# Value projection of all heads ahead of the attention, as seven half-size products; the r projection gated afterwards

## The chip, the cores and the metric

The kernel runs on one core of one Trainium2 chip. The metric is the device time of one launch in microseconds (us). The core has TensorE (PE in the profile; its weight loads are PEld), VectorE (DVE), ScalarE (ACT), GpSimd (POOL) and SyncE (SP), which in this kernel issues the transfers. Each engine executes its instructions in the order in which the program lists them; waits between engines go by semaphores.

## The reference, cut to what matters

One encoder block over 1024 tokens with 1024 features, all in float32:

```python
h = rmsnorm(x, norm_mix)
q, k, v, r, lr_f, lr_b, u, g_a, g_b = split(h @ w_in)     # q, k: 512 wide; v, r: 1024 wide
log_a = log_sigmoid(lr @ w_decay_up + b_decay) / 16       # one set forward, one backward
o = gla(q, k, v, log_a_f) + flip(gla(flip(q, k, v, log_a_b)))   # 4 heads, q/k 128 and v 256 wide per head
o = o * rsqrt(mean(o * o) + eps) * gla_norm * silu(r)
y_a = o @ w_branch_gla
y_b = (multiscale_pool(u) @ w_pool_group) * pool_scale
x = x + (sigmoid(g_a) * y_a + sigmoid(g_b) * y_b) @ w_out
h2 = rmsnorm(x, norm_ffn)
x = x + (silu(h2 @ w_gate) * (h2 @ w_up)) @ w_ffn_out
out = rmsnorm(x, norm_final)
```

Products are taken to float32 accuracy: each operand is split into a high part (a cast to float32r) and a low part (the difference), and three matmuls add high x high, high x low and low x high.

## The kernel before

Tokens are in tiles of 128. `mm3` issues the three matmuls of one 128-deep step and then calls `pump`, which takes the clock for all work that runs beside the products: with every step it lowers the counters of waiting pieces by the width of the step over 512 columns (below: a unit). Three lists are served: `side` (generators such as `attention`, one after the other, each `yield` naming the units until its next piece), `aside` (preparations, one job per so many units) and `put_off` (`soon`: one piece after so many units). So the order of instructions on every engine is fixed when the program is written.

The stages, in order:

1. Start. Token tiles are normalized, transposed on PE and split into `hT` (feature-major, high and low). Meanwhile the value product of head 0 runs token tile by token tile: `values` takes 8 steps of 256 columns for a tile (head 0 has 256 value columns), each step three matmuls, and `split_to` casts the sum on ACT and subtracts on DVE. `low_rank_weights` prepares the decay weights behind tile 5; tiles 6 and 7 and then the low-rank product (L449) follow.
2. Heads. For each head `project_qk` makes q and k (4 groups of 8 steps of 512 columns), then `attention(h)` begins as a side generator. It runs beside the next head's q, k and values, and for the last head beside r. Its chain: four products `z`, then on DVE a minimum (L644), on ACT Abs, Exp, Ln with an activation table load (L645, L650, L656), then per half and direction a DVE subtraction (L663), a scan (L670, L675), and the ends of it (L681); ACT Exp twice (L688, L689), DVE and POOL multiplications (L696, L697); PE transposes of keys (L714), a split of them (`kt`, L198), the state recurrence over 8 tiles (`advance`: three matmuls `kv`, L728, L733), scores, outputs `op`.
3. r. For each of 8 column tiles `feature_major` multiplies; `gated` applies Silu on ACT to the sum, transposes the attention's output on PE and multiplies on DVE (L979); results go to HBM (`ob_out`). Beside it `feature_jobs` restores `hT` (high + low) and forms the sums and differences of its quadrants that the following stages need (DVE, L600), casts (L594) and subtracts (L585); they stay in SBUF (`right`).
4. Gates (10 units of 256 columns), branch product, output product, FFN in, FFN out. All of these already use Winograd's form of Strassen's algorithm: seven products of half size in place of eight, with operand sums formed beside and result sums kept in PSUM or added on DVE. Product numbers 1 to 7 in the code are those seven; 1, 6, 7 and 4 share one PSUM sum (`UP`).

Weights come by SP from HBM (`raw`), are cast on ACT (L197, `wh`) and their low part is subtracted on POOL (L198, `wl`). PSUM has 8 banks: 3 in the pool `ps_mm`, 5 in `ps_g`. SBUF work tiles come from a pool of 39 slots of 4 KB per partition. SP's transfers go round eight semaphores: a transfer waits until the eighth before it has landed.

Of the kernel before, what the change touches and what calls it, by code (L numbers as in the profile page):

```python
# [17 lines left out]
P = 128  # L18
# [33 lines left out]
def kernel(  # L52
# [182 lines left out]
    order = []  # L235
    for h in range(HEADS):
        cols_of = [(Q0 + h * DK, DK), (K0 + h * DK, DK), (V0 + h * DV, DV)]
        order += [(w_in, KT, *c) for c in (cols_of if h else cols_of[2:] + cols_of[:2])]
    order += [(w_in, KT, R0 + j * P, P) for j in range(KT)]
    order = iter(order)  # L240
# [25 lines left out]
    mm_banks = cycle([ps_mm])  # L266
# [92 lines left out]

    load_x(0)  # L360
# [4 lines left out]
    fetch()  # L365
# [38 lines left out]
    def value_slots():  # L404
        return [(slot(F32R, (4, DV), "vh"), slot(F32R, (4, DV), "vl")) for _ in range(2)]

    v = value_slots()
# [13 lines left out]
    prepare()  # L421
    for kp, ps in enumerate(trs):
        pending.pop(0)()
        gain_and_split(ps, kp, 0, hT, g_mix)
    w = take(ahead=False)
    norm_x(2)
    norm_x(3)
    for t in range(0, NT, 2):
        if t + 4 < NT:
            begin(norms(t + 4), 1)  # L430
# [6 lines left out]
        if t + 2 < NT:  # L437
            begin(to_features(xn[(t + 2) % 4 :], t + 2, hT, g_mix), 0.5)
        values(w, v, t + 1)
        finish_side()  # L440
        if t == 4:
            low_rank_weights()
    prepare()
    lrT = slot(F32R, (2, HALF), "lrT")
    for half in range(2):
        ps = bank(ps_mm)
# [43 lines left out]

    def chunk(w, k_half, c_half, c):
        k0 = (4 * k_half + 2 * c) * P
        return w[k0 : k0 + 2 * P, c_half * HALF : (c_half + 1) * HALF].rearrange("(k p) c -> p k c", p=P)

# [48 lines left out]
    def feature_jobs(c):  # L543
        def restored(i, j):
# [7 lines left out]
        b12, job = restored(0, 1)  # L552
        yield job
        b11, job = restored(0, 0)
        yield job
        yield diff(b11, b12, b11)
        b22, job = restored(1, 1)
        yield job
        yield diff(b12, b22, b12)
        yield diff(b22, b22, b11, 6)  # L560
        yield None, b12, 7
        yield None, b11, 5
        b21, job = restored(1, 0)
        yield job
        yield diff(b21, b21, b22, 4)
# [6 lines left out]
    def beside(jobs, every, put, lag):  # L572
# [3 lines left out]
        while True:  # L576
            job = next(jobs, None)
            if not any((job, *casts, differ, *puts)):
                return
            for pair in puts.pop(0):  # L580
                nc.sync.dma_start(*pair)
            puts.append([])
            if differ:
                src, (hi, lo), dst = differ
                nc.vector.tensor_tensor(lo, src, as_f32(hi), op=ALU.subtract)  # L585
                if len(src.shape) == 2:
                    puts[-1] += [(dst[:, i, :], as_f32(t)) for i, t in enumerate((hi, lo))]
                else:
                    right.setdefault(dst, []).append((hi, lo))
            differ, cast = None, casts.pop(0)  # L590
            if cast:
                src, dst = cast
                parts = parts_for(src)
                nc.scalar.copy(parts[0], src)  # L594
                differ = src, parts, dst
            casts.append(None)
            if job:
                op, src, dst = job
                if op:
                    op()  # L600
# [17 lines left out]
    v_heads, o_heads, unscaled = {}, {}, []  # L618
    HOLD, SCORES = 4.4, 6

    def project_qk():
        q = slot(s="q")
        k = slot(s="k")
        for dst, scale in ((q, DK**-0.5), (k, 1.0)):
            w = take()
            for half in range(2):
                ps = feature_major(w, hT, half)
                nc.scalar.activation(dst[:, half, :], ps[:, :], AF.Copy, scale=scale)
        return q, k

    def attention(h, q, k):


        qe = [slot(s="qe") for _ in range(2)]
        ke = [slot(s="ke") for _ in range(2)]
        fac = {}
# [47 lines left out]
        def exponentials(half, d):  # L684
            cs, tot, e_q = zs[half, d], totals[half, d], qe[half]
# [7 lines left out]
        def apply_decay(half, d):  # L693
            f, e_q, e_k = fac[half, d], qe[half], ke[half]
# [61 lines left out]
        yield HOLD - 2  # L756
        exponentials(0, 1)
# [10 lines left out]
        while h not in v_heads:  # L768
            yield 0.5
# [80 lines left out]
    for h in range(HEADS):  # L850
        qk = project_qk()
        begin(attention(h, *qk))
        if h == 0:
            prepare_beside(map(branch_jobs, range(4)), 6)
        if h > 0:
            v = value_slots()
            w = take()
            for t in range(NT):
                values(w, v, t)
        v_heads[h] = v  # L860
# [103 lines left out]
    raw_r, oT = [], {}  # L964

    def gated(j, half, src):

        sr = t2(s="sr")
        nc.scalar.activation(sr[:, :], src, AF.Silu)
# [6 lines left out]
        if j // 2 not in oT:  # L976
            oT[j // 2] = [slot(s="o") for _ in range(2)], []
        tiles, there = oT[j // 2]
        nc.vector.scalar_tensor_tensor(  # L979
            tiles[half][:, j % 2, :], tp[:, :], g_gla[:, j : j + 1], sr[:, :], op0=ALU.mult, op1=ALU.mult  # L980
        )
        there.append((j, half))
        if len(there) == 4:
            c = j // 2 % 2
            for half, t in enumerate(tiles):
                later(ob_out[j // 4, half][:, 2 * c : 2 * c + 2, :], t[:, :, :])

    def put_by():

        if raw_r:  # L990
            gated(*raw_r.pop(0))

    BY = 3
    sums_begun = False
    for j in range(KT):
        if 2 <= j <= 4:
            load_o(j - 2)
        w = take()
# [3 lines left out]
        if j == 7:  # L1002
            gates_ahead.step()
        if j < BY:
            whole_r = slot(s="r")
        for half in range(2):
            if j >= BY and not sums_begun and (j > BY or not side):
                finish_side()
                finish_beside()
                prepare_beside([feature_jobs(0), feature_jobs(1)], 2.3)  # L1010
                sums_begun = True
            ps = feature_major(w, hT, half)
            if half == 0:
                flush()
            if j < BY:
                nc.scalar.copy(whole_r[:, half, :], ps[:, :])
                raw_r.append((j, half, whole_r[:, half, :]))
            else:
                put_by()
                gated(j, half, ps[:, :])  # L1020
            if j == KT - 1 and half == 0:
                gates_ahead.step()
    finish_beside()
# [58 lines left out]

    def weight_split(raw):
        parts = []
        for k in range(2):
            hi = wts.tile([P, HALF], F32R, tag="wh", name=name("wh"))
            lo = wts.tile([P, HALF], F32R, tag="wl", name=name("wl"))
            split_to(hi[:, :], lo[:, :], raw[:, k, :], nc.gpsimd)
            parts.append((hi[:, :], lo[:, :]))
        return parts  # L1090
# [242 lines left out]

    U_BANKS = [ps_mm] * 3 + [ps_g]
    X_BANKS = [ps_g] * 4
# [534 lines left out]
```

## Time and profile before

| | |
|---|---|
| runs | 1396.67, 1399.2, 1400.53 us, median 1399.2 |
| profiled execution | span from first to last instruction 1400.4 us, which the page gives as its time |
| PE busy | 1371.4 us (98%) |
| DVE, ACT, POOL busy | 854.4, 624.6, 750.4 us (61%, 45%, 54%) |
| transfers | 243.62 MB, mean 174 GB/s |

The page gives busy time per engine over the span, the chain of work that ended last, and groups of equal instructions by line and tile name with count, busy time, mean duration of one, and the idle time before them. Matmuls overlap in the records: the step from one start to the next, which the merged rows of the chain give (time over count), is what one costs in a stream.

### The profile page before, as it was taken

How to read it: one execution, taken by the hardware profiler on the slowest of the kernel's cores; microseconds unless marked ns; L12 is line 12 of the kernel's file. 1: busy time of each engine (PE TensorE's matmuls, PEld its weight loads, DVE VectorE, ACT ScalarE, POOL GpSimd, SP SyncE). 2: the span in 40 equal slices, each digit the busy share in tenths (PEclk: the TensorE clock that was granted, in tenths of full speed). 3: DMA queues.
4: the chain of work that ended last, by engine and by line, in shares of the span. 5: the costliest groups of instructions: out<-in, count | busy, mean ns of one | idle time of the engine just before them, and what ended most of it. 6: DMA issues, size and time to landing. Idle time of an engine off the chain costs nothing.

```text
span 1400.4 us, 18571 instructions
## 1 busy us (share of the span) xinstructions
PE 1371.4 (98%) x6677; PEld 1157.4 (83%) x6677; DVE 854.4 (61%) x1073; ACT 624.6 (45%) x1119; POOL 750.4 (54%) x558
## 2 busy tenths in 40 slices
PE   7999999999999999999999999999999999999997
PEld 6889898988888878788887888888888888888876
DVE  6256857677745975587874865556565556343363
ACT  6364655554334444455346633333333334453253
POOL 3251616132288456468665176666666667454354
PEclk9999999999999999999999999999999999999999
DMA  6212413222368667996524455554444447975461
GB/s 193 76 45 61 136 59 107 89 79 71 125 207 286 199 220 235 346 407 233 194 76 173 173 180 174 173 173 156 145 142 148 140 153 255 388 255 218 165 234 67
DMA packets 167612, 243.62 MB, mean 174 GB/s; under 512 B 10936, under 2 KB 98016, under 8 KB 167520
## 3 DMA queue, kind: packets, MB, share of 16 engines
q1 hardware_dynamic: 167520, 242.45, 51.2%
q8 instruction: 52, 0.85, 0.2%
q14 instruction: 40, 0.33, 0.1%
HBM read 164.55 MB, written 77.86 MB: 173 GB/s over the span
## 4 chain that ended last, share of the span: by engine, by line
PE 81%; DVE 7%; ACT 4%; issue 3%; POOL 2%; DMA 2%; SPq 0%; POOLq 0%; DVEq 0%; ACTq 0%
PE ps L271 73%; PE op L813 2%; POOL wl L198 1%; PE kv L271 1%; PE sc L741 1%; PE op L271 1%; DVE z L670 1%; PE yb L271 1%; PE tr L318 1%; PE ps L449 1%; PE tp L972 1%; DMA gor<-g_out 0%; DMA wor<-t_out 0%; DVE z L675 0%; DMA u_out<-uph 0%
## 5 line engine op out<-in xcount | busy, mean ns | idle before, releaser
L198 POOL TENSOR_TENSOR wl<-fs,wh 128x512 fp32r<-128x512 f32 x120 | 165.9, 1386 | 163.4 <-ACT wh L197 138.1
L271 PE MATMUL ps<-gl,wh 128*128 128x512 f32 x616 | 239.8, 389 | 0.9 <-DVE gl L1462 0.9
L271 PE MATMUL ps<-gh,wh 128*128 128x512 f32 x616 | 240.4, 390 | 0.0
L271 PE MATMUL ps<-gh,wl 128*128 128x512 f32 x616 | 239.7, 389 | 0.0
L198 POOL TENSOR_TENSOR wl<-fraw,wh 128x512 fp32r<-128x512 f32 x90 | 129.1, 1435 | 63.9 <-ACT wh L197 63.9
L271 PE MATMUL ps<-hh,wh 128*128 128x512 f32 x376 | 150.4, 400 | 0.0
L198 POOL TENSOR_TENSOR ol<-gor,oh 128x1024 fp32r<-128x1024 f32 (+1 forms) x42 | 100.3, 2394 | 93.1 <-ACT oh L197 86.0
L271 PE MATMUL ps<-hh,wl 128*128 128x512 f32 x376 | 146.9, 391 | 0.0
L271 PE MATMUL ps<-hl,wh 128*128 128x512 f32 x376 | 146.8, 390 | 0.0
L198 POOL TENSOR_TENSOR wl<-raw,wh 128x512 fp32r<-128x512 f32 x47 | 64.4, 1382 | 152.8 <-ACT wh L197 141.4
L271 PEld LDWEIGHTS ps<-gl,wh 128*128 128x128 f32 x616 | 115.7, 188 | 25.0 <-DVE gl L1462 1.3
L271 PEld LDWEIGHTS ps<-gh,wl 128*128 128x128 f32 x616 | 115.7, 188 | 24.2
L271 PEld LDWEIGHTS ps<-gh,wh 128*128 128x128 f32 x616 | 115.7, 188 | 23.6
L271 PE MATMUL ps<-oh,oh 128*128 128x512 f32 x308 | 119.9, 389 | 1.3 <-DVE x L1792 1.3
L271 PE MATMUL ps<-ol,oh 128*128 128x512 f32 x308 | 119.9, 389 | 0.2 <-DVE ol L198 0.2
L271 PE MATMUL ps<-oh,ol 128*128 128x512 f32 x308 | 119.8, 389 | 0.0
L198 POOL TENSOR_TENSOR wl<-wraw,wh 128x512 fp32r<-128x512 f32 x56 | 90.9, 1653 | 45.4 <-ACT wh L197 36.1
L198 DVE TENSOR_TENSOR ol<-wor,oh 128x1024 fp32r<-128x1024 f32 (+1 forms) x42 | 62.0, 1496 | 53.9 <-ACT oh L197 46.6
L197 ACT CAST wh<-fs 128x512 fp32r<-128x512 f32 x120 | 73.8, 615 | 28.4 <-DVE fs L882 28.3
L271 PEld LDWEIGHTS ps<-hh,wl 128*128 128x128 f32 x376 | 70.8, 188 | 15.3
L271 PEld LDWEIGHTS ps<-hl,wh 128*128 128x128 f32 x376 | 71.1, 189 | 13.5
L271 PEld LDWEIGHTS ps<-hh,wh 128*128 128x128 f32 x376 | 71.1, 189 | 13.2
(251 smaller groups left out, 3197.4 us busy)
## 6 DMA issues: line engine op xcount, KB each, us to landing
fraw<-in_w_ffn_in_dram SPq DMA_DIRECT2D x44, 512.0 KB, 6.1
gor<-g_out SPq DMA_DIRECT2D x35, 512.0 KB, 6.3
raw<-in_w_in_dram SPq DMA_DIRECT2D x48, 256.0 KB, 3.1
g_out<-s SPq DMA_DIRECT2D x44, 256.0 KB, 2.3
fraw<-in_w_in_dram SPq DMA_DIRECT2D x20, 512.0 KB, 6.5
wor<-t_out SPq DMA_DIRECT2D x20, 512.0 KB
g_out<-g SPq DMA_DIRECT2D x33, 256.0 KB, 2.6
x<-in_x_dram SPq DMA_DIRECT2D x16, 512.0 KB, 4.9
```

The source lines that it names most:

```text
L197: nc.scalar.copy(hi, src)
L198: eng.tensor_tensor(lo, src, as_f32(hi), op=ALU.subtract)
L271: nc.tensor.matmul(ps, a[i], b[j], start=first and n == 0, stop=last and n == 2, skip_group_check=onto)
L318: nc.tensor.transpose(ps[:, c], xt[:, k * P : (k + 1) * P], ident[:, :])
L449: nc.tensor.matmul(ps[:, :], lw[k // 4][:, k % 4, :, :].rearrange("p a r -> p (a r)"), hT(k, half)[i], start=k == 0 and i == 0, stop=k == ...
L670: nc.vector.tensor_tensor_scan(cs[:, :], cy, la[:, :], 0.0, op0=ALU.mult, op1=ALU.add)
L741: nc.tensor.matmul(sc[d][:, i * CH : (i + 1) * CH], chunk_of(ke, n, d), chunk_of(qe, n, d), start=True, stop=True,)
L813: nc.tensor.matmul(op[:, :DV], a, b, start=False, stop=j == len(terms) - 1)
L972: nc.tensor.transpose(tp[:, i * P : (i + 1) * P], o_heads[j // 2][half][:, i, (j % 2) * P : (j % 2 + 1) * P], ident[:, :],)
```

## The change

The value product moves ahead of the attention for all four heads together, as one 1024 x 1024 x 1024 product in seven products of half size.

- Products 1 and 2 use weights as they are in memory and the first half of the tokens. They take the place of `values` in the start (`early`, 4 token tiles, each 4 steps of 512 columns per product). Product 1's sums stay in PSUM (three banks of `ps_mm`, one of `ps_g`) and are copied; `first_block` adds product 2 to the copy, which finishes one quadrant of the values.
- Then the low-rank product and q, k of head 0, half by half. `low_rank_weights` now stands behind the last `first_block`. Beside the second half `feature_jobs` starts (DVE): the sums of weight blocks in place, and the sums of `hT`.
- Then products 5, 3, 6, 7, 4 in that order (`VALUES`), each 2 parts of 4 token tiles and 2 steps. 6, 7 and 4 add on top of product 1's sums, so each must wait until `out_values` has read the sum before (DVE add), has cast it (ACT) and made its low part (DVE). `attention` of head 0 begins with product 6.
- The finished values go to HBM as high and low parts (`v_out`), and each head loads its own (`load_values`, 4 transfers) in the middle of its attention.
- The split feature sums that were made for products 5, 6, 7, 4 also go to HBM (`t_out_h`) and are loaded again just before the gates (`load_right`, 16 transfers of 512 KB).
- r is projected without its gate: r 0 to 2 behind q, k of head 2, r 3 to 7 behind head 3. r 0 to 5 go to HBM. A side generator `gating` begun after r 6 loads r and the attention outputs, applies Silu to a whole r tile and does what `gated` did.

The diff, cut to its core:

```diff
-    def values(w, v, t):
-        ps = bank(ps_mm)
-        for kt in range(KT):
-            mm3(ps[:, :DV], tokens(hT(kt, t // 4), t), w(kt), kt == 0, kt == KT - 1)
-        split_to(*(part[:, t % 4, :] for part in v[t // 4]), ps[:, :DV])
+    def early(p, t, w):
+        ps = U.setdefault(t, bank(U_BANKS[t])) if p == 1 else bank(ps_g)
+        for k in range(4):
+            mm3(ps[:, :], tokens(hT(k + 4 * (p == 2), 0), t), w[k], k == 0, k == 3)
+        return ps
...
+    def first_block(t, p1, hi, lo):
+        ps = early(2, t, w2)[:, :]
+        m = t % 2
+        nc.vector.tensor_tensor(ps, ps, p1[:, m, :], op=ALU.add)
+        nc.scalar.copy(hi[:, m, :], ps)
+        nc.vector.tensor_tensor(lo[:, m, :], ps, as_f32(hi[:, m, :]), op=ALU.subtract)
...
-        values(w, v, t + 1)
+        hi, lo = slot(F32R, s="vh"), slot(F32R, s="vl")
+        for m in range(2):
+            first_block(t + m, p1, hi, lo)
         finish_side()
-        if t == 4:
-            low_rank_weights()
+        soon(2, partial(store_values, 0, t, hi, lo))
+    low_rank_weights()
...
+    def first_qk(half):
+        if half == 0:
+            begin(to_features(xn[2:], 6, hT, g_mix), 2)
+        else:
+            finish_side()
+            prepare_beside([feature_jobs()], 1.5, 6)
+        low_rank(half)
+
+    qk = [project_qk(first_qk)]
+    VALUES = (5, 3, 6, 7, 4)
...
+    def out_values(i, half, m, ps, s=None):
+        hi, lo = v_parts[i, half][m // 2]
+        m2 = m % 2
+        if s is not None:
+            add(lo[:, m2, :], ps, s[:, m2, :])
+            ps = lo[:, m2, :]
+        nc.scalar.copy(hi[:, m2, :], ps)
+        def low():
+            nc.vector.tensor_tensor(..., ps, as_f32(hi[:, m2, :]), op=ALU.subtract)
+        soon(1.5, low)
+        if m2:
+            soon(5, partial(store_values, i, 4 * half + m - 1, hi, lo))
...
+    for at, p in enumerate(VALUES):
+        if p == 5:
+            x_banks = [bank(pool) for pool in X_BANKS]
+        elif p == 6:
+            begin(attention(0, *qk[0]))
+        sums = x_banks if p in (5, 3) else [U[m] for m in range(4)]
+        for c in range(2):
+            n = 2 * at + c
+            while len(split_v) <= n:
+                next_values()
+            next_values()
+            for m in range(4):
+                for k in range(2):
+                    mm3(sums[m][:, :], tuple(t[:, k, m * P : (m + 1) * P] for t in data), split_v[n][k], ...)
...
-    for h in range(HEADS):
-        qk = project_qk()
-        begin(attention(h, *qk))
-        if h > 0:
-            v = value_slots()
-            w = take()
-            for t in range(NT):
-                values(w, v, t)
-        v_heads[h] = v
+    for h in range(1, HEADS):
+        q, k = project_qk()
+        begin(attention(h, q, k))
+        if h == 2:
+            for j in range(3):
+                project_r(j)
...
+    def load_right(p):
+        right[p] = []
+        for c in range(2):
+            parts = [slot(F32R, s=s)[:, :, :] for s in ("trh", "trl")]
+            for i, t in enumerate(parts):
+                nc.sync.dma_start(as_f32(t), t_out_h[p][:, c, i])
+            right[p].append(parts)
+
+    for j in range(3, KT):
+        project_r(j)
         if j == 6:
             for _ in range(2):
                 gunits[0].load()
+            finish_beside()
+            begin(gating())
...
+    for p in (5, 6, 7, 4):
+        load_right(p)
```

More of the change, by code (lines that the diff above doesn't have):

```diff
@@ L693, in apply_decay @@
         def apply_decay(half, d):
+            if half not in ke:
+                ke[half] = slot(s="ke")
             f, e_q, e_k = fac[half, d], qe[half], ke[half]
@@ L756, in attention @@
         yield HOLD - 2
+        while h // 2 not in values_out:
+            yield 0.5
+        load_values(h)
         exponentials(0, 1)
@@ new lines, with project_r @@
+    settle()
+    finish_beside()
+    right.clear()
+    mm_banks = cycle([ps_mm])
+    prepare_beside(map(branch_jobs, range(4)), 6)
+    KEPT, kept = 6, {}
+    r_out = [dram.tile([P, 2, HALF], F32, name=f"r_out{j}") for j in range(KT)]
+    def project_r(j):
+        w = take()
+        r = slot(s="r")
+        for half in range(2):
+            ps = feature_major(w, hT, half)
+            if half == 0:
+                flush()
+            nc.scalar.copy(r[:, half, :], ps[:, :])
+        if j < KEPT:
+            later(r_out[j], r[:, :, :])
+        else:
+            kept[j] = r
@@ L1001 @@
                 gunits[0].load()
-        if j == 7:
+            finish_beside()
+            begin(gating())
+        elif j == 7:
             gates_ahead.step()
[L1004 to L1023, printed above, removed]
+            gates_ahead.step()
+    while len(side) > 1:
+        next(side[0][0], None) is None and side.pop(0)
+    for p in (5, 6, 7, 4):
+        load_right(p)
     for p, i, half in ((1, 0, 0), (2, 1, 0), (3, 1, 1)):
@@ L1081, in weight_load @@
         return raw
[L1083 to L1090, printed above, removed]
     def data_split(src):
```

271 lines of the change are left out of this document (188 added, 83 removed).

## The prediction

> **What bounds the kernel now.** I read the page's first part, the chain that ended last, the chain in order of time, and then the stretches in which the change works.
>
> ```profile
> span 1400.4 us, 18571 instructions
> PE 1371.4 (98%) x6677; PEld 1157.4 (83%) x6677; DVE 854.4 (61%) x1073; ACT 624.6 (45%) x1119; POOL 750.4 (54%) x558
> PE 81%; DVE 7%; ACT 4%; issue 3%; POOL 2%; DMA 2%; SPq 0%; POOLq 0%; DVEq 0%; ACTq 0%
> ```
>
> PE is the bound, and 81% of the chain is matmuls. Busy PE is not PE at its peak, so I take the step between starts from streams without a gap (start, time, instruction, count):
>
> ```profile
> 38.98 6.11 PE ps L271 x51
> 334.23 0.88 PE tp L972 x8
> 390.44 78.92 PE ps L271 x348
> ```
>
> A matmul with 256 columns costs 6.11/51 = 119.8 ns, one with 512 columns 78.92/348 = 226.8 ns, a transpose 0.88/8 = 0.11 us. The last stream runs 79 us without a break, so what is taken off PE comes off the time, unless a wait takes its place. Around the change PE hardly waits, but DVE is nearly full in the middle of an attention (columns: stretch, its length, PE, PEld, DVE, ACT, POOL busy, clock, DMA share, GB/s):
>
> ```profile
> 52.00:74.00 22.00, 22.00 (x99) 18.22 (x98) 0.69 (x1) 4.45 (x8) 5.08 (x4) 1.00 0.37 108
> 84.00:102.00 18.00, 18.00 (x103) 15.72 (x102) 15.01 (x24) 11.81 (x25) 13.13 (x11) 1.00 0.15 45
> PE kv L271 <- DVE kt L198: 3.4, 3, 2.1
> ```
>
> The first row is q and k of head 0 alone, the second attention 0, DVE busy 15.0 of 18 us. The third, from the waits of PE between 74 and 325 us, is its largest there: 3.4 us in three waits for DVE.
>
> **The change, part by part.**
>
> *Less PE work.* The values were 8 tiles x 4 heads x 8 steps x 3 = 768 matmuls of 256 columns; their rows:
>
> ```profile
> L271 PE MATMUL ps<-wh,hh 128*128 128x256 f32 x256 | 79.9, 312 | 0.0
> L271 PE MATMUL ps<-wl,hh 128*128 128x256 f32 x256 | 73.3, 286 | 0.5 <-POOL wl L198 0.5
> L271 PE MATMUL ps<-wh,hl 128*128 128x256 f32 x256 | 73.0, 285 | 0.0
> ```
>
> Now 7 products x 4 tiles x 4 steps x 3 = 336 matmuls of 512 columns. 768 x 0.1198 = 92.0, 336 x 0.2268 = 76.2: **-15.8 us**. Everything else on PE stays in number.
>
> *New preparations.* The rows that price them (busy, mean ns; then idle before):
>
> ```profile
> L600 DVE TENSOR_TENSOR hs<-hs,hs 128x1024 f32<-128x1024 f32 x8 | 11.8, 1481 | 0.2
> L600 DVE TENSOR_TENSOR hs<-hh,hl 128x1024 f32<-128x1024 f32 x8 | 10.7, 1351 | 0.0
> L585 DVE TENSOR_TENSOR trl<-hs,trh 128x1024 fp32r<-128x1024 f32 x8 | 10.6, 1342 | 8.6 <-DMA ob_out<-o 5.6 <-ACT trh L594 3.1
> L644 DVE TENSOR_SCALAR la<-z,cols 128x512 f32<-128x512 f32 x16 | 11.7, 746 | 22.4 <-PE z L641 22.4
> L663 DVE TENSOR_TENSOR la<-la,z 128x512 f32<-128x512 f32 x16 | 10.8, 678 | 7.7 <-ACT z L656 7.7
> L670 DVE TENSOR_TENSOR_SCAN z<-carry,la 128x512 f32<-128x512 bf16 x8 | 14.4, 1802 | 0.3
> L675 DVE TENSOR_TENSOR_SCAN z<-la,carry 128x511 f32<-128x511 f32 x8 | 13.8, 1731 | 0.3
> L681 DVE TENSOR_TENSOR z<-z,tot 128x256 f32<-128x256 f32 x16 | 6.9, 432 | 0.5
> L696 DVE TENSOR_TENSOR ke<-z,k 128x512 f32<-128x512 f32 x16 | 10.9, 680 | 0.0
> L198 DVE TENSOR_TENSOR kt<-kp,kt 128x512 fp32r<-128x512 f32 x16 | 11.0, 691 | 16.3 <-ACT kt L197 16.3
> 402.34 0.68 DVE L1256 TENSOR_TENSOR ga<-ps,ga 128x512 f32<-128x512 f32 x1
> L197 ACT CAST wh<-raw 128x512 fp32r<-128x512 f32 x48 | 28.8, 620 | 1.2 <-DMA raw<-in_w_in_dram 1.2
> L645 ACT ACTIVATE z<-z,cols 128x512 f32<-128x512 f32 x16 | 10.5, 662 | 9.1 <-DVE la L644 8.9
> L650 ACT ACTIVATE z<-z 128x512 f32<-128x512 f32 x16 | 8.2, 582 | 0.0
> L594 ACT CAST trh<-hs 128x1024 fp32r<-128x1024 f32 x8 | 8.1, 1048 | 18.9 <-DMA ob_out<-o 8.3 <-PE tp L972 6.5 <-DVE hs L600 4.2
> L656 ACT ACT_TABLE_LOAD x4 | 5.1, 1283 | 0.1
> L628 ACT ACTIVATE k<-ps 128x512 f32<-128x512 f32 x8 | 4.8, 595 | 10.9 <-PE ps L271 10.9
> L399 ACT CAST lw<-lraw 128x384 fp32r<-128x384 f32 x2 | 0.9, 530 | 0.0
> L198 POOL TENSOR_TENSOR wl<-raw,wh 128x512 fp32r<-128x512 f32 x47 | 64.4, 1382 | 152.8 <-ACT wh L197 141.4 <-issue 8.4 <-PE kv L271 3.0
> ```
>
> *Start.* PE begins behind the same chain of POOL subtractions. It now has 24 matmuls of 512 columns before it wants token tile 2, not of 256, but that tile's transfer stands behind twice the weights: -2 to +3, I take **-1**.
>
> *Low-rank weights, now behind the last value sum.* The low-rank product waits for a DVE addition (0.68), the cast (0.6, as L628), the low part (0.69, while ACT casts `lw`, 0.53) and the low part of `lw` (0.28, an estimate from L681's size): 2.25, with four handovers **+2.5** (1.5 to 3). Before, tiles 6 and 7 covered it.
>
> *First weights of product 5.* Their casts stand on ACT behind the last k sum, and nothing is split ahead: k 0.6, cast 0.62, two POOL subtractions 2 x 1.38 = 3.98, then two more matmuls, 4.4 with handovers, where four token tiles could have had 1.36 for the first: **+3.1** (2 to 3.5). Later weights are one part (5.4 us) ahead and POOL needs 2.8, so they cost nothing.
>
> *Products 6, 7 and 4 beside attention 0.* Here I expect the loss. Product 7 may not add to a PSUM sum before DVE has read product 6's, and product 4 likewise; those additions stand on DVE between the attention's instructions. From the first `la` to the last addition that product 4 waits for, DVE has 4 la (3.0), 4 subtractions (2.7), 4 scans (7.1) with ends (1.7 + 0.7), 3 ke (2.0), 1 kt (0.7), and newly 4 low parts of feature sums (5.4), 8 additions (5.4) and 6 low parts of values (4.1): 32.9 us. PE without waits reaches that point 10.9 (product 6) + 10.9 (7) + 4.1 (three tiles of 4) + 4 z (0.9), 8 transposes (0.9) and 3 kv (0.4) = 28.1 us after product 6 began. DVE also comes late by some 2.5 us: the feature and weight sums (24 pieces of 1.35 to 1.48, 8 low parts of 1.34 in all) occupy it from the low-rank product on. So 2.5 + 32.9 - 28.1 = 7.3 us if DVE never waited. It does wait: its low parts need casts that stand on ACT behind 4 Abs (2.6), 4 Exp (2.3), 4 Ln (2.3, as L650), the table (1.3), two feature casts (2.1) and weight casts (1.2), 12 us in a row, and again behind the Exp pairs. Following both queues in the program's order, the fourth tile of product 7 starts 24 us after product 6 began, not 16, and the fourth of product 4 some 48 instead of 28: 20 us. Durations overlap a little from start to start, so **+17** (7 to 24). Queued behind: the first `kv`, its load of values, q and k of head 1; the attention runs on beside q and k of head 1 and r, where DVE has room again, so nothing more is lost.
>
> *Heads 1 to 3.* DVE and ACT lose the splits of values (24 of 32), so the 3.4 us of PE's waits for `kt` may go: **-3.4** (0 to -4). The value loads are issued some 10 units (7 us) ahead of use; I take nothing, up to +3.
>
> *r and gates.* r's products and transposes are as many as before. The 33 us of DVE work of `feature_jobs` (both L600 rows and L585) leave a stage in which PE did not wait: nothing. What is new is the transfers: 16 loads of 512 KB = 8.4 MB just before the gates, beside r (3 MB each way) and behind `ob_out`.
>
> ```profile
> 390.00:410.00 20.00, 20.00 (x92) 16.61 (x90) 10.41 (x10) 7.79 (x14) 17.79 (x13) 1.00 0.74 233
> 410.00:430.00 20.00, 20.00 (x90) 16.54 (x89) 7.92 (x8) 6.91 (x13) 19.84 (x15) 1.00 0.94 261
> 570.00:600.00 30.00, 30.00 (x128) 24.52 (x127) 18.77 (x23) 16.51 (x28) 14.78 (x12) 0.96 1.01 380
> ```
>
> At the best rate here, 380 GB/s, 8.4 MB take 22.1 us, in a stage that already kept the transfers busy for 0.74 to 0.94 of the time. Product 5 of unit 0 wants the first quarter 2.7 us after the gates begin, product 6 the next 2.7 us on, and the weights of unit 1 are queued on SP behind all 16. If the loads begin 5 us early, 22.1 - 5 - 8 (products 1, 2, 3 of unit 0, which need none) = 9: **+7** (0 to 14).
>
> Sum: -15.8 - 1 + 2.5 + 3.1 + 17 - 3.4 + 7 = +9.4. The profiled span is 1.2 us over the median of the runs, so I set the sum on the median: 1399.2 + 9.4 = 1408.6, **1409 us**.
>
> **The rivals.**
>
> *The PE gain shows (faster).* It decides at one point: if DVE's additions keep up, so that products 7 and 4 wait no more than 4 us together, and the loads of the gates cost 4: -15.8 - 1 + 5.6 + 4 - 3.4 + 4 = -6.6, 1393 us. For it: the attention's pieces are spread with pauses, and DVE is free in the stretch before (0.69 of 22 us, above). Against: 32.9 us of DVE work in 28.1 of PE's.
>
> *Gain and waits cancel.* With 12 us of waits in products 7 and 4 and 4 at the gates: +1.4, 1401 us.
>
> *DVE and POOL keep each other off.* The same DVE subtraction takes 681 ns at the median and up to 1720; one of 1.77 us lies over POOL subtractions of 1.7:
>
> ```profile
> L882 DVE TENSOR_TENSOR fs<-fs,fraw x30: 674/681/1720, 385.5 to 1158.4; 128x512 f32<-128x512 f32 x30
> 408.37 1.77 DVE L882 TENSOR_TENSOR fs<-fraw,fraw 128x512 f32<-128x512 f32 x1
> 409.56 1.73 POOL L198 TENSOR_TENSOR wl<-fraw,wh 128x512 fp32r<-128x512 f32 x1
> ```
>
> In products 6, 7 and 4 POOL has 10 weight subtractions and 4 multiplications, 20 of some 40 us, and 10 of the new DVE instructions read SBUF twice: 10 x 0.5 x (1.77 - 0.68) = 5.5 us; the 12 feature sums beside products 5 and 3 bring another 6, of which half lasts: 1409 + 9 = 1418 us. [...]
>
> *The gates wait for all 8.4 MB:* +14 in place of +7, 1416 us.
>
> **How the numbers follow.** Forecast 0.42, port 0.13, gates 0.08, cancel 0.13, faster 0.24. A change under 0.3% (4 us) is about what a measurement of this kernel can't tell from none. Slower 0.42 + 0.13 + 0.08 = 0.63, same 0.13, faster 0.24. The range runs from the faster case (1393, less 5 for its own bounds) to the port case (1418, with 8 for wider waits): 1388 to 1426; the forecast's own is 1402 to 1426.
>
> **What would show it.** Right: no 256-column `ps` groups and 336 more of 512 columns; PE waits for DVE `vs` additions in products 7 and 4, 10 us or more together; a gap of some 2.5 us before the low-rank product and 3 before product 5; PE waits for `t_h` loads or the next unit's weights where the gates begin. Wrong: PE without gaps in products 6, 7 and 4, or new waits of heads 1 to 3 for `v_out` loads.

## The result, and the profile after

The changed kernel takes 1448.3 us (median of 4 runs, 1446.7 to 1453.0) against 1397.9 us (1396.6 to 1400.5) for the kernel before, run beside it: a ratio of 1.0365, 95% interval 1.0343 to 1.0387. It is 50 us slower. The forecast was 1409 us, slower by 9, with a range up to 1426: the sign was right, the size was not.

The page of the changed kernel, first part:

```profile
span 1445.0 us, 17902 instructions
PE 1374.7 (95%) x6245; PEld 1132.0 (78%) x6245; DVE 875.0 (61%) x1078; ACT 640.9 (44%) x1127; POOL 767.7 (53%) x567
PE 53%; DVE 5%; issue 2%; POOL 2%; DMA 2%; ACT 1%; SPq 0%; POOLq 0%; DVEq 0%; ACTq 0%
```

PE has 432 matmuls fewer, as forecast, but its busy share falls from 98% to 95%. The chain in the last line could be followed back only to 505 us, so it says nothing of the stages that were changed. The transfers of one execution rise from 243.6 to 284.5 MB. The waits of PE (us in total, times, longest):

```profile
PE ps L274 <- ACT wh L197: 18.1, 4, 8.2
PE ps L274 <- DVE vs L968: 7.9, 6, 2.0
PE ps L274 <- POOL wl L198: 7.0, 11, 1.2
...
PE kp L806 <- DVE ke L788: 4.2, 1, 4.2
PE ps L499 <- DVE lw L430: 3.0, 1, 3.0
```

The largest row, 18.1 us for casts of weights, has no counterpart before. I took every step from one matmul's start to the next in both traces, subtracted the step at full clock (226.8 ns for 512 columns, 119.8 for 256), and put the rest down to half clock where the clock's record shows that PE was granted half its clock, to waits otherwise. Summed by stages of the span (us):

| stage (after) | before: waits + half clock | after: waits + half clock | difference | forecast |
|---|---|---|---|---|
| 0 to 79: start, low rank, q and k of head 0 | 7.7 + 1.4 | 13.5 + 2.9 | +7.3 | +1.5 |
| 79 to 106: products 5 and 3 | 0.2 + 0 | 2.2 + 2.8 | +4.8 | +3.1 |
| 106 to 160: products 6, 7, 4 beside attention 0 | (attentions below) | 18.0 + 4.1 | +22.1 | +17 |
| 160 to 180: weights of head 1 | | 8.9 + 1.7 | +10.5 | 0 |
| 180 to 400: heads and r (before: 106 to 400) | 20.0 + 1.5 | 18.6 + 1.7 | -1.2 | -3.4 |
| 400 to 460: first gates | 0 + 0 | 13.3 + 3.4 | +16.7 | +7 |
| 460 to the end | 14.4 + 1.6 | 15.0 + 0 | -0.9 | 0 |

Together +59.3, where the two spans differ by 1445.0 - 1400.4 = 44.6; so some 14.8 us less are left for PE's own work (forecast 15.8). The rows are good to some 2 us, because next to a matmul of another width a step differs from that in a stream (in the changed kernel the step from a matmul of 128 columns to one of 512 is 29 ns at the median of 56, among matmuls of 128 columns it is 109): with such short and long steps set off against each other, the row of the heads is +0.9 and that of the gates +15.4. Of the 59.3, 47.2 are waits and 12.1 are time at half clock, which no term of the forecast had.

Two of the waits for casts are about 8 us long. The first, in order of time (start, length, engine, line, instruction; in brackets the idle time before it and what ended it):

```profile
168.16 0.39 PE L274 MATMUL ps<-wh,trl 128*128 128x512 f32 x1
169.92 0.64 SPq L468 DMA_DIRECT2D v_out<-vl  x1
170.61 3.82 SPq L205 DMA_DIRECT2D raw<-in_w_in_dram  x4
175.86 0.62 ACT L197 CAST wh<-raw 128x512 fp32r<-128x512 f32 x1 [6.69 <-DMA raw<-in_w_in_dram]
176.53 0.79 PE L274 MATMUL ps<-hh,wh 128*128 128x512 f32 x1 [7.99 <-ACT wh L197]
```

Product 4 ends at 168.5. The weights of head 1 (L205) stand on SP behind the last stores of values, which stand behind the last low part on DVE; asked for at 170.6, they let the first cast start 5.3 us later. ACT and PE only pass the wait on. The DMA share is 1.02 between 168.6 and 173.8 us, so this is the time of a transfer beside others.

The second, with the DMA share in stretches around it (columns: stretch, length, busy PE, PEld, DVE, ACT, POOL, granted clock, DMA share, GB/s):

```profile
420.00:430.00 10.00, 8.17 (x33) 6.28 (x32) 7.12 (x7) 5.40 (x9) 8.49 (x6) 0.83 1.01 409
430.00:441.00 11.00, 11.00 (x50) 9.12 (x49) 0.00 (x0) 1.69 (x3) 1.68 (x2) 1.00 1.03 404
441.00:450.00 9.00, 0.82 (x4) 0.40 (x3) 0.00 (x0) 0.62 (x1) 1.50 (x2) 0.64 1.06 344
```

```profile
414.73 0.40 SPq L1199 DMA_DIRECT2D trh<-t_h  x1
...
431.56 0.32 SPq L1199 DMA_DIRECT2D trl<-t_h  x1
432.78 1.60 SPq L162 DMA_DIRECT2D ob_out<-o  x2
435.39 1.56 SPq L544 DMA_DIRECT2D wsum<-in_w_out_dram  x2
437.90 5.39 SPq L1058 DMA_DIRECT2D fraw<-in_w_in_dram  x2
449.01 0.62 ACT L197 CAST wh<-fraw 128x512 fp32r<-128x512 f32 x1 [15.04 <-DMA fraw<-in_w_in_dram]
449.68 0.80 PE L274 MATMUL ps<-hh,wh 128*128 128x512 f32 x1 [8.18 <-ACT wh L197]
```

The transfers are full from 420 to 450 us (share 1.01 to 1.06); the DMA view gives, for 414 to 447 us:

```profile
DMA packets 4363, 12.16 MB, mean 368 GB/s; under 512 B 361, under 2 KB 1546, under 8 KB 4362
```

The weights of gate unit 1 stand behind all 16 reloads, then `ob_out` and `w_out`. The reloads themselves are in time (PE has no wait for `t_h`); it stops at the next unit.

### The profile page after: what moved, and what is told of

Read it like the earlier page. It is cut to its first block, busy times and chain, and to the rows that moved or that the text cites. A ratio compares the mean times of both kernels' runs of the same rounds, so it can differ in the third digit from the quotient of the medians.

```text
span 1445.0 us, 17902 instructions
## 1 busy us (share of the span) xinstructions
PE 1374.7 (95%) x6245; PEld 1132.0 (78%) x6245; DVE 875.0 (61%) x1078; ACT 640.9 (44%) x1127; POOL 767.7 (53%) x567
## 4 chain that ended last, share of the span: by engine, by line
PE 53%; DVE 5%; issue 2%; POOL 2%; DMA 2%; ACT 1%; SPq 0%; POOLq 0%; DVEq 0%; ACTq 0%
PE ps L274 52%; DVE fs L1066 1%; DMA u_out<-uph 1%; POOL wl L198 1%; DVE ws L1232 1%; PE yb L274 1%; DVE ws L1226 0%; DVE ga L1439 0%; DMA gor<-g_out 0%; DMA wor<-t_out 0%; DVE x L1726 0%; POOL n3rs L1709 0%; POOL mg L1348 0%; POOL gl L1642 0%; ACT hb L1660 0%
## 5 line engine op out<-in xcount | busy, mean ns | idle before, releaser
L274 PE MATMUL ps<-hh,wh 128*128 128x512 f32 x376 | 157.4, 419 | 16.9 <-ACT wh L197 16.9
L198 POOL TENSOR_TENSOR wl<-raw,wh 128x512 fp32r<-128x512 f32 x32 | 42.0, 1326 | 141.3 <-ACT wh L197 133.8
```

The lines of the kernel that those rows point to most:

```text
L198: eng.tensor_tensor(lo, src, as_f32(hi), op=ALU.subtract)
L274: nc.tensor.matmul(ps, a[i], b[j], start=first and n == 0, stop=last and n == 2, skip_group_check=onto)
```

## The experiments

Each time stands beside the kernel before, run on the same chip (1397.5 to 1400.0 us); the changed kernel's ratio is 1.0365. Between chips the times differ by 2 us or so, so differences of a few us are better read from the ratios.

**1. The order of SP's queue: weights ahead of stores.**

```
+ if p == 7 and c == 0: fetch(); fetch()      # q, k of head 1
+ if p == 4 and c == 1: prepare()
```

> Edit: the transfers of the q and k weights of head 1 are issued when product 7 begins, and the first of them is split during product 4, instead of both behind the last value stores on SP's queue. Theory (queue order): PE's 8.1 us wait for those weights at 176.5 us is SP standing at the v_out stores, which wait for the last casts and low parts; it falls under 1 us, and with it the stretches at half clock around it (about 2 us of time): 1448.3 - 10 = 1438 us. Rival (nothing to do meanwhile is not the point, the attention is): attention 0 on DVE and ACT is what is late, so head 1 waits as long at its kv or kt instructions: 1446 to 1449 us.

1438.5 us, ratio 1.0289 (1.0273 to 1.0304): the 10 us that queue order gives. The 8 us wait is gone and head 2's remains. Then one weight further ahead for all heads:

```
  ready.append(Weights(loaded.pop(0)))
+ if qk_done and not loaded: fetch()
```

> Edit: the weights of head 1 asked for early (as in the first run, 1438.5 us), and from then on the raw weights of q, k and r are asked for one weight further ahead. Theory: PE's 3.7 us wait for ke at 239 us, and what follows it, is ACT standing in order at the cast of head 2's k weights, whose transfer stands on SP behind the o_out stores, and those behind DVE's normalizing; asked for ahead of the stores it costs under 1 us: 1438.5 - 4 = 1434 us. Rival (less cover: attention 1 lacks the value matmuls it once ran beside, so DVE and ACT are late in themselves): 1437 to 1439 us, with the wait still there.

1430.1 us, 1.0227 (1.0211 to 1.0242). Head 2's wait, of the changed kernel, was of the same kind:

```profile
222.14 3.52 SPq L515 DMA_DIRECT2D o_out<-o  x2
228.48 1.09 SPq L205 DMA_DIRECT2D raw<-in_w_in_dram  x2
235.57 0.62 ACT L197 CAST wh<-raw 128x512 fp32r<-128x512 f32 x1 [8.59 <-DMA raw<-in_w_in_dram]
238.61 0.69 DVE L788 TENSOR_TENSOR ke<-z,k 128x512 f32<-128x512 f32 x1 [8.01 <-ACT z L779]
```

A cast that stood 8.6 us for its weights held the exponentials behind it on ACT, those held `ke` on DVE, and PE waited 4.2 us. With the weights early, that row is gone from the waits. So queue order at two places cost 18 us, and the rival, that attention lacks the cover of the value matmuls, falls for these two waits.

**2. The gates: order or bytes?**

```
  for p in (5, 6, 7, 4):
      load_right(p)
+     if p == 6: gunits[1].load(); gunits[1].load()
```

> Edit: the two transfers with the weights of gate unit 1 are issued between the reloads of products 6 and 7, not behind all 16 reloads and the ob_out stores. Theory (queue order on a full DMA): the 8.2 us wait of PE at 449.7 us goes, and the half clock behind it (about 2 us), because the 16 reloads are needed one product after another and the transfers run at 410 GB/s: 1448.3 - 10 = 1438 us. Rival (bandwidth): 8.4 MB in a stage that is already full must be paid somewhere; products 7 and 4 of unit 0 then wait for t_h reloads, together about as long: 1445 to 1449 us.

1452.8 us, 1.0395 (1.0375 to 1.0416): nothing gained, both expectations missed. PE's wait of unit 1 grew (waits of this kernel, then two rows of POOL in order of time):

```profile
PE ps L274 <- POOL wl L198: 19.1, 11, 11.7
```

```profile
451.73 1.26 POOL L670 TENSOR_TENSOR wsum<-wsum 128x512 f32<-128x512 f32 x1 [18.33 <-DMA wsum<-in_w_out_dram]
452.95 1.26 POOL L198 TENSOR_TENSOR wl<-fraw,wh 128x512 fp32r<-128x512 f32 x1
```

The weights were there, but their low part stood on POOL behind a preparation of `w_out`, whose transfer was now the last in the row. So that was moved too:

```
- if n == 0: prepare_beside(map(output_jobs, range(4)), 2.8)
+ if n == 1: prepare_beside(map(output_jobs, range(4)), 2.8)
```

> Edit: the weights of gate unit 1 between the reloads of products 6 and 7, as before, and the preparations of w_out, which POOL makes beside the gates, begun with unit 1 instead of unit 0. Theory: in the run with the weights alone moved, PE waited 11.7 us for a POOL low part that stood behind a sum of wsum, whose transfer was behind the reloads; with both moved the wait of unit 1 falls under 1.5 us, and its half clock (2 us) goes: 1448.3 - 9 = 1439 us. Rival (bandwidth): the same wait comes back at products 7 or 4 of unit 0, or at unit 2's weights: 1445 to 1450 us.

1446.6 us, 1.0342 (1.0325 to 1.0360). The wait of unit 1 is gone, and 6.4 us of waits appear between 460 and 540 us, where there were 0.6: the rival. From here on the base is the run with 1430.1 us. On it, the same with the preparations begun after five products of unit 0:

> Edit: on top of the run with the weights asked for deeper (1430.1 us), the weights of gate unit 1 between the reloads of products 6 and 7, and the preparations of w_out begun after five products of unit 0 instead of before the first. Theory (queues): the 9.7 us wait of unit 1 and its 2.3 us at half clock go, and less than 2 us come back later in unit 1 to 3: 1430 - 10 = 1420 us. Rival (bandwidth, as the run with both moved gave 1446.6 us: the time came back as waits at 500 to 535 us): 1427 to 1431 us.

1427.5 us, 1.0194 (1.0171 to 1.0218); and with the reloads of products 7 and 4 themselves put off:

```
- for p in (5, 6, 7, 4): load_right(p)
+ for p in (5, 6): load_right(p)
...
+ if n == 0 and at in (1, 3): load_right(7 if at == 1 else 4)
```

> Edit: on top of the run with the weights asked for deeper (1430.1 us), only the gates' part of the combined run: reloads of products 7 and 4 asked for after the second and fourth product of unit 0, the preparations of w_out after its fifth product. Theory: as without the reloads, 9 to 12 us less: 1420 us. Rival (bandwidth): half of it comes back in units 1 to 3 as in the two runs before it that only changed the order (1427.5 us).

1432.5 us, 1.0239 (1.0222 to 1.0256): no gain. Order gives 0 to 3 us, by the ratios up to 5. Then 12 of the 16 reloads left out:

```
- for p in (5, 6, 7, 4): load_right(p)
+ load_right(5)
+ for p in (6, 7, 4): right[p] = right[5]
```

> Edit: on top of the run with the weights asked for deeper (1430.1 us), the gates load the feature sums of product 5 alone and use them in products 6, 7 and 4 too, so 12 of 16 reloads (6.3 MB) are left out and the values of the gates are not the reference's; all matmuls stay. Theory (the reloads are what unit 1's weights stand behind): the 9.7 us wait and its 2.3 us at half clock go: 1418 us. Rival (the ob_out stores, which wait for the gating, hold the queue by themselves): 1426 us or more.

1415.5 us, 1.0117 (1.0099 to 1.0134): 14.6 us less; waits and half clock between 400 and 460 us fall from 15.6 to 2.7 us. The same stretches of the base and of this kernel:

```profile
420.00:440.00 20.00, 10.70 (x37) 7.88 (x36) 7.24 (x7) 4.60 (x8) 10.56 (x8) 0.74 0.94 307
```

```profile
420.00:440.00 20.00, 20.00 (x90) 16.57 (x89) 7.82 (x8) 7.03 (x13) 19.84 (x15) 1.00 0.89 269
```

PE goes from 10.7 busy of 20 to 20.0. It is the bytes: every order I tried had to bring them through a stage whose transfers are full (a share of 1.01 from 414 to 447 us in the changed kernel, 1.02 from 400 to 420 us in the base).

**3. Products 6, 7 and 4 beside attention 0.** The additions and low parts left out of `out_values`:

```
- if s is not None:
-     add(lo[:, m2, :], ps, s[:, m2, :])
-     ps = lo[:, m2, :]
  nc.scalar.copy(hi[:, m2, :], ps)
...
- soon(1.5, low)
```

> Edit: products 6, 7 and 4 keep their matmuls, their casts on ACT and their stores, but the 8 additions and 12 low parts on DVE are left out (the values are then not the reference's). Theory (DVE in order): the six waits of PE for these additions (7.9 us in products 7 and 4) fall under 2 us, some 2 us of half clock go too, and head 1's weights are asked for some 8 us sooner: 1448.3 - 8 - 2 - 3 = 1435 us. Rival (ACT in order): the casts stand on ACT between Abs, Exp and Ln, so PE waits as long for the casts instead: 1446 to 1449 us.

1443.1 us, 1.0328 (1.0312 to 1.0343), between the two. DVE's 7.9 us of waits are gone, and PE waits for a cast on ACT instead, in the rows of this kernel:

```profile
PE ps L274 <- ACT vh L967: 3.7, 1, 3.7
```

```profile
122.33 1.28 ACT L744 ACT_TABLE_LOAD   x1
123.62 2.05 ACT L744 ACTIVATE z<-z 128x512 f32<-128x512 f32 x4
125.55 2.09 ACT L967 CAST vh<-ps 128x512 fp32r<-128x512 f32 x4
```

This wait is the edit's own. In the changed kernel the cast and the low part of products 6 and 7 read the sum that the addition has left in SBUF (`ps = lo`), so the next product waits for the addition alone, and not for cast and low part too, as "The change" has it. Without the addition the cast reads PSUM, and PE must wait for it. In the changed kernel ACT holds PE up only by way of DVE, which stands at a low part until its cast is done while the next addition is behind it:

```profile
123.91 0.69 DVE L973 TENSOR_TENSOR vs<-vs,vh 128x512 fp32r<-128x512 f32 x1 [1.80 <-ACT vh L970]
```

So the run shows that the additions were in the way; what ACT's order costs it doesn't show. On the base the attention itself was then moved:

```
- begin(attention(0, *qk[0]))
+ begin(attention(0, *qk[0]), 24)
```

> Edit: on top of the run with the weights asked for deeper (1430.1 us), attention 0 begins 24 steps of three matmuls (16 us) later, in the middle of product 7. Theory (attention 0 and the sums of values share DVE's and ACT's order): the waits inside products 7 and at the start of 4 (5 us and a half clock) go, those in product 4 stay, and the heads behind have room to take the attention: 1430 - 5 = 1425 us. Rival: the collision only moves, to product 4 and head 1, and the attentions end later, beside r and the gating: 1430 to 1434 us.

1424.5 us, 1.0177 (1.0161 to 1.0192). Waits and half clock between 106 and 160 us fall from 20.8 to 9.7 us, but PE loses some 6 us more than the base at product 5 and behind product 4. Matmul by matmul it is 4 to 5 us ahead of the base before the gates and 1.6 us ahead after them: some 3 us are given back there. PE now stops once at the gates, 14.7 us (9.1 in the base), because the gating ends later and its stores stand behind the reloads:

```profile
PE ps L276 <- ACT ga L1442: 16.9, 3, 14.7
```

```profile
417.60 1.41 DVE L1168 SCALAR_TENSOR_TENSOR o<-tp,cols,r 128x512 f32<-128x512 f32 x2 [15.98 <-DMA ob_out<-o]
```

Whether the two are separate losses, the later attention without the reloads tells (with product 5's weights split early, as below):

> Edit: the run that leaves 12 of the 16 reloads out (1415.5 us, the gates' values are not the reference's), with attention 0 from the middle of product 7 and product 5's first weights split ahead. Theory (the places add up once the gates' stage no longer gives anything back): 12 to 15 us of waits in products 7 and 4 and 2 us at product 5 go, head 1's load of values costs 4: 1415.5 - 12 = 1403 us, level with the kernel before or just over it. Rival (the later attention is paid beside r and the gating, whatever the reloads do): 1413 to 1416 us.

1404.2 us, 1.0042 (1.0028 to 1.0056), as the theory had it: 11.3 us more, product 5's share included, and nothing given back at the gates, where 1.9 us of waits are left. Even so it is no faster than the kernel before.

**4. Sums on POOL in place of DVE.** The eight sums of weight blocks moved, two `add` and six `sub`:

```
- yield partial(add, block(1, 1, c), ...)
+ yield partial(padd, block(1, 1, c), ...)
```

> Edit: on top of the run with the weights asked for deeper (1430.1 us), the eight sums of weight blocks (128x1024) go from DVE to POOL. Theory (DVE in order is what makes the additions of products 6 and 7 late): DVE is relieved of 8 x 1.7 to 2.0 = 15 us ahead of attention 0, and PE's waits in products 6 to 4 (8.8 us for additions) fall by some 4: 1426 us. [...]

1431.9 us, 1.0226 (1.0210 to 1.0241): no difference. With 13.7 us taken off DVE, what stayed took longer. DVE's feature sums between 50 and 110 us, in the changed kernel and in this run, and the moved sums on POOL:

```profile
L670 DVE TENSOR_TENSOR hs<-hh,hl 128x1024 f32<-128x1024 f32 x8 | 11.9, 1488 | 0.0
```

```profile
L672 DVE TENSOR_TENSOR hs<-hh,hl 128x1024 f32<-128x1024 f32 x7 | 14.1, 2016 | 1.2 <-POOL wl L198 1.2
L672 POOL TENSOR_TENSOR wv<-wv,wv 128x1024 f32<-128x1024 f32 x8 | 20.9, 2626 | 0.3
```

The rows of this kernel have DVE's other feature sums at 1950 ns (`hs<-hs,hs`, x7), where the changed kernel has 1518. So 14 sums that stayed on DVE took 0.53 and 0.43 us longer each, 6.7 us together, in a stretch in which POOL had 20.9 us of the moved ones, and PE's waits for the additions are 9.0 us, in the base 8.8. The trace of before has such a difference too: DVE's subtraction `fs<-fraw,fraw` (128x512) took 0.68 us at the mean in 19 cases with POOL's instructions over less than a tenth of it, 1.65 us in 9 with POOL over more than 0.6 of it; `ga<-ps,ga`, which reads PSUM, took 0.68 us (9 cases) and 0.69 (20). What makes the difference isn't shown. The move gained nothing; it isn't where the 50 us went.

**5. The start and product 5.** The split of the low-rank weights ahead of product 2 of tiles 2 and 3, then the same without the decay rows (`up`):

```
  load_wv(1, 0); load_wv(1, 1)
+ low_rank_weights()
  hi, lo = slot(F32R, s="vh"), slot(F32R, s="vl")
```

> Edit: the split of the low-rank weights is moved ahead of product 2 of token tiles 2 and 3, instead of behind their last value sum. Theory: the 3.2 us wait of PE before the low-rank product goes to under 0.5, and the 6.8 us at half clock behind it (2.9 us of time) go too: 1448.3 - 6 = 1442 us. Rival: the casts and low parts only push the value sums back by as much, and the product 2 or the stores wait: 1447 to 1449 us.

> Edit: as in the run that moved the low-rank weights, but only the two casts and two low parts of lw are moved ahead of product 2 of tiles 2 and 3; the cast of the decay rows (up), for whose transfer ACT stood 3.8 us there, stays behind. Theory: PE's 3.0 us wait for lw goes to under 0.5 us, and the 2.9 us that the 6.8 us at half clock behind it cost go with it: 1448.3 - 6 = 1442 us. Rival: the wait before the low-rank product is the value sums' own chain on DVE and ACT, and the product waits as long for a bank or for hl: 1447 to 1449 us.

1452.1 us, 1.0391 (1.0373 to 1.0408), and 1451.5 us, 1.0383 (1.0366 to 1.0400). The first made ACT stand 3.8 us for the decay rows. In the second the wait for `lw` is gone, and another lay under it (ACT in order of time, then PE):

```profile
50.35 0.62 ACT L197 CAST wh<-raw 128x512 fp32r<-128x512 f32 x1 [0.19 <-DMA raw<-in_w_in_dram]
50.88 2.29 ACT L328 ACTIVATE hh<-tr,cols 128x256 fp32r<-128x256 f32 x6
51.74 1.66 DVE L331 SCALAR_TENSOR_TENSOR hl<-tr,cols,hh 128x256 fp32r<-128x256 f32 x4 [5.20 <-ACT hh L328]
52.76 0.45 PE L321 MATMUL tr<-ident,xn 128*128 128x128 f32 x1 [5.34 <-DVE hl L331]
```

The q weights of head 0 land late, and `hh` of the last tiles stands behind their casts. With those asked for first:

```
+ fetch(); fetch()
  for d, w_up in enumerate((w_decay_up_fwd, w_decay_up_bwd)):
```

> Edit: as in the run with lw split early (1451.5 us, where ACT then stood at the casts of q of head 0 until 50.9 us and PE waited 5.3 us for hl behind them), and the q and k weights of head 0 asked for ahead of the decay rows and the four value blocks. Theory: two waits lay one under the other, lw and the q weights, whose transfer stands behind 2 MB; with both moved PE's 6 us of waits and 2.9 us of half clock between 36 and 53 us go: 1448.3 - 7 = 1441 us. Rival: the value blocks, now later, hold the feature sums and product 5 back by as much: 1447 to 1450 us.

1448.0 us, 1.0363 (1.0346 to 1.0380). The trace shows product 5's first wait at 76.8 us instead of 80.3, so 3.4 us were gained there. Of these, 2.6 are left at 366 us, and by 375 us PE is 0.5 us behind the changed kernel: the gain is lost ahead of the gates, in the attention of head 3 (waits for `kt` and the state of 0.2, 0.3 and 1.6 us). Why they appear in this run stays open. Unit 1 starts at 450.2 us, no earlier than in the changed kernel. Product 5's first weights split ahead of the last k sum, on the base:

```
  if n % 2 == 0: before(half)
+ elif n == 3: next_values()
```

> Edit: on top of the run with the weights asked for deeper (1430.1 us), the first half of product 5's weights is split before the last k sum instead of behind it. Theory: PE's waits at 79 to 84 us (1.4, 1.2, 1.0 us and the half clock of 1.6 us behind them) fall to the second half's alone, under 1 us: 1430 - 4 = 1426 us. Rival: DVE's feature sums, 24 of 27 us busy there, hold product 5 or 3 next: 1429 to 1431 us.

1427.7 us, 1.0199 (1.0182 to 1.0216): 2.4 us of the 4 by the times, 3.9 by the ratios.

**6. Gaps filled, and everything together.** Matmuls of no use in three gaps:

```
+ stay_busy(12, ps_g)    # before the low-rank product
+ stay_busy(32, ps_mm)   # before q of head 1
+ stay_busy(32, ps_g)    # before gate unit 1
```

> Edit: three of PE's gaps are filled with matmuls of no use (12 before the low-rank product, 32 before q of head 1, 32 before gate unit 1; 76 x 0.227 = 17 us of extra matmuls inside gaps of 3.2, 8.2 and 8.2 us). Nothing else changes, the waits behind them stay. Theory (PE's own idleness halves the clock for some time after): no half clock behind these gaps, which cost 2.9, 1.9 and 1.9 us: 1448.3 - 6 = 1442 us. Rival (the half clock has another cause, or the gaps' cost is only their length): 1448 us or more.

1449.1 us, 1.0365 (1.0350 to 1.0380). 17 us of matmuls cost nothing, so the gaps are real; but half clock went from 16.6 only to 15.5 us, since other gaps (2.5 us at 50.3 us, 3.1 us at 448.7) took its place. Behind the three gaps themselves the record of the clock had 6.8, 6.8 and 10.2 us at half clock, and with the gaps filled 3.4 us each, as the theory says; in products 6, 7 and 4 it grew. So the time is the rival's, and the run doesn't price the clock. All the orders that helped, together (the weights early and deeper, product 5 split, attention 0 later, the reloads of products 7 and 4 put off, the preparations of `w_out` later):

> Edit: everything that gave time, together: weights asked for early and deeper, product 5's first weights split ahead, attention 0 from the middle of product 7, the reloads of products 7 and 4 asked for after the second and fourth product of the first gate unit, and the preparations of w_out after the fifth. Theory (each place is a queue in order, and the gates' transfers were what gave back the later attention's gain): from 1424.5 us the 14.7 us wait of the gates goes to 3, and product 5 gives 2: 1410 us, still over the kernel before by the start, the low-rank gap and product 5's rest. Rival (the stage holds its transfers only just: 8.4 MB of reloads beside ob_out, w_out and unit weights): the wait goes to products 7 and 4 of the gates or to units 1 to 3, 1420 to 1425 us. If it comes below 1396 us the change pays after all.

1420.6 us, 1.0159 (1.0143 to 1.0175): the rival. The gates wait for the late reloads themselves:

```profile
PE ps L276 <- DMA trh<-t_h: 4.9, 1, 4.9
```

No version that computes all of it came under the kernel before.

## Why the prediction was wrong

Three things went about as forecast. *Less PE work* is some 14.8 us against 15.8. *Products 6, 7 and 4* were named as a place of loss: 22.1 us there against 17 (7 to 24). But the 17 were waits for DVE's additions, and of those PE has 7.9 us, less than the 10 that were to show it; 2.8 more are waits for POOL's low parts, 3.3 for `kt` and the state, 4.1 are half clock, and some 4 stand in no row of the waits. So the nearness of the sum is in part luck; without the additions and low parts, and with a wait of 3.7 us for a cast in their place, the kernel gained 5.2 us. *Heads 1 to 3*: the waits for `kt` behind 180 us are 1.0 us instead of 3.4, as forecast, but the row gave only 1.2, or nothing, because of head 2's weights (below). PE never waited for a `v_out` load in the changed kernel (it did, 3.9 us, when the attention came later).

The step that failed is the end of the paragraph on products 6, 7 and 4: "Queued behind: the first `kv`, its load of values, q and k of head 1; ... so nothing more is lost". I listed head 1's weights as queued and then priced them at nothing, because I followed DVE's and ACT's order and not SP's. The store waits for the last low part, the weights wait for the store, and a transfer takes 5.3 us: 10.5 us, and the undoing gave 9.8. Head 2's weights, behind `o_out`, gave 8.4 more in the second run; that stage, which came out level with the kernel before, could have been 7 us under it (180 to 400 us: 20.3 us of waits and half clock in the changed kernel, 13.5 in the second run).

*r and gates* was mis-sized: +7 (0 to 14), measured 16.7, and 14.6 came back without 12 of the reloads. The mechanism of the rival "the gates wait for all 8.4 MB" was nearer, and it had 0.08. I had written that unit 1's weights are queued behind all 16 loads, and summed the wait of unit 0's products instead; the 8 us of cover that I took for products 1, 2 and 3 don't fit that either, since of these only product 1 stands ahead of products 5 and 6. The transfers ran at 404 to 409 GB/s at their best, better than the 380 that I took; but `ob_out` and `w_out` stood in the same row, and 12.2 MB moved between 414 and 447 us, not 8.4.

Last, every wait was priced at its own length. Half clock makes 16.6 us after and 4.5 before: 2.9 follow the low-rank gap alone (forecast 2.5; the wait itself took 3.0), and the table has the rest. The trace of before had it beside the longest wait that I quoted, in these stretches:

```profile
229.30:231.20 1.90, 0.00 (x1) 0.00 (x0) 0.76 (x2) 1.32 (x4) 1.05 (x2) 1.00 0.50 131
231.20:234.60 3.40, 3.20 (x11) 2.81 (x12) 3.23 (x6) 1.02 (x2) 3.32 (x4) 0.50 0.20 77
```

The forecast had 25.2 us of losses, the table has 59.3. Of the 34.1 between them, 10.5 are head 1's weights, 9.7 the gates, 5.1 products 6 to 4, 5.8 the start, 1.7 product 5, 2.2 the heads, -0.9 the rest.

By the runs, 18.2 us (weights asked for early), 14.6 (reloads) and 11.3 (attention 0 later, product 5 split) make 44.1 of the 50. The last two were measured with gates whose values are not the reference's, so they show where the time is and not a kernel that could be used. The rest, the start's waits above all, is open.

## What to carry to other kernels

When a stage gets new stores, follow SP's queue to the next transfer that PE needs, and price a late transfer at its whole time to landing (here 5.3 us from the issue to the first cast), plus what stands on ACT and POOL behind its cast. Where the transfers are already full, count all bytes up to the next needed one, not only the new ones: here a change of order moved such a wait (0 to 3 us gained by the times), and only fewer bytes took it away (14.6 us). And ask of a saving of matmuls whether PE has other work ready: here 15 us saved met 59 us of waits and half clock.

## What the runs showed of the hardware

In the 19 profiles of this case the granted clock changed only at the ends of stretches of 3.41 us, and what it became went with how busy PE had been in the stretch before. In each profile the changes lie whole multiples of 3413.33 ns apart, to 2 ns (1.3 in that of the changed kernel, 0.6 in that of before). Cut into such stretches from the clock's first record on, and counted for those at full clock, PE's busy share and the clock of the next one are, in all profiles and in those of before and after alone:

```
                       all 19 profiles                     before and after
PE busy in a stretch   stretches   next one at half clock  stretches   next one at half clock
under 0.4                 74          74                       6           6
0.4 to 0.5                67          45                       9           6
0.5 to 0.6                62           3                       6           1
over 0.6                7481           0                     786           0
```

So two waits of 1 us in one stretch were enough in the changed kernel: waits of 1.2 and 0.9 us end at 80.3 and 81.7 us, PE was busy for 0.38 of the stretch from 78.3 us on, and half clock followed from 81.7 us on. At half clock a matmul of 512 columns started 427 ns after the one before (median in before and after), at full clock 226.8. My estimate from this and the table: a wait of 2 us costs another 3.41 x (1 - 226.8/427) = 1.6 us, or nothing, by where it falls.
